# A decoder layer in split fp32: up blocks split in one piece, another order of pairs and plain blocks, and a pair's sums moved back by a unit

## The chip, the cores and the metric

The kernel runs on one core of one Trainium2 chip. The metric is the device time of one execution in microseconds; the median of three runs stands for a kernel. The profile shows one further execution, taken with the hardware profiler.

## The reference

One layer of a causal decoder with 256 tokens and 1024 channels in fp32: three attention mixers are merged, followed by a residual layer norm, a feed-forward part and a second layer norm. Only the feed-forward part and what lies around it bear on this change:

```python
x = layer_norm(ALPHA * x + merged @ w_out[i], ln1_g[i], ln1_b[i])
h = jnp.square(jax.nn.relu(x @ w_up[i])) @ w_down[i]        # w_up 1024 x 4096, w_down 4096 x 1024
ple = jax.nn.sigmoid(x @ w_ple_gate[i]) * (p[i] @ w_ple[i])
x = layer_norm(ALPHA * x + h + ple, ln2_g[i], ln2_b[i])
```

## The kernel before

**Split numbers.** Every fp32 matrix is written as a high part, rounded by a copy to fp32r, and a low part, the rest. A product is three matmuls: high by high, high by low, low by high. A *unit* is a piece of 128 rows by up to 1024 columns of weights. `Weights._split` loads it to a tile `raw` (SyncE's queue), ScalarE casts it to `whi`, and VectorE (for the later units of the kernel alone) subtracts to get `wlo`. There are five buffers each of `raw`, `whi` and `wlo`; `W.get(i)` asks for the splits up to four units ahead of the one that TensorE is about to use.

**The up stage (`for f in range(32)`).** For each of the 32 blocks of 128 hidden channels TensorE does eight matmuls of 512 columns with `whi` as the stationary operand (L929) and eight of 256 columns with `wlo` (L932). VectorE adds the parts (L913), ScalarE applies relu and square, and the result is split into `hT[f]`. The parts of an up unit lie in their tiles at columns given by `UP`: `(16, 192, 320, ...)` for `whi` and `(64, 208, 336, ...)` for `wlo`. The first block of 128 columns stands away from the seven others, so `Apart.runs` gives two runs, and the cast (L109) and the subtraction (L122) of a unit are two instructions each, of 256 and 768 columns.

**The down stage.** The 32 row blocks of `w_down` are used in the order `SEQ`, then `LATE` (26 to 31). Seven *pairs* of row blocks, the tuples of `SEQ`, go through a scheme with seven products in place of eight; the other blocks are *plain*. A plain block is one unit, four products, 12 matmuls of 512 columns. A pair is four units (three of 1024 columns, one of 512), seven products, 21 matmuls. Its units are not all weights as loaded: `load(i)` brings the two row blocks of pair `i` into half of `xr` by three DMAs (L882, L884), and `form(i)` makes the sums and differences by three VectorE instructions (L891 with 1024 columns, L892 and L893 with 512) into `wt[i]` and `xr`. The pair's four units are then split from `wr[i][:, 1]`, `wt[i][:, 0:1024]`, `wr[i][:, 0]` and the last 512 columns of `wt[i]` (L111 and L118). So the second unit needs `form(i)`, the first doesn't. `xr` takes the place of `x1`, the input of the up stage, and has room for two pairs; `load(i + 2)` must wait until pair `i` has been split. It is asked for through the list `later`, when the last unit of pair `i` is split, and `form(i + 2)` is written right behind it.

**The end.** Eight accumulators `P[1]` to `P[8]` collect the products. Behind block 23 VectorE adds them up (`plus`, L1003); meanwhile TensorE does half of the products of blocks 24 and 25 (onto `P[3]` and `P[2]`). The other half goes onto `P[4]` and `P[8]`, and can start when these adds are done. Then come the blocks of `LATE` and the second layer norm.

**Order.** A planner orders each engine's instructions by readiness and program order under its own estimate of durations. `tc.issue_after(x)` keeps what is written in its block behind instruction `x` in the order of `x`'s engine.

Of the kernel before, what the change touches and what calls it, by code (L numbers as in the profile page):

```python
# [142 lines left out]
def hybrid_layer(ctx: ExitStack, tc: tile.TileContext, x0, xn, pT, wqk, wva, wvb, wg, wbc, wba,  # L143
# [12 lines left out]
    W = Weights(tc, raw, part)  # L156
# [75 lines left out]
    def add(*a, at=(0, 0), by=DV):  # L232
        i = n_u[0]
        n_u[0] += 1
        return W.add(*a, by=by if i < 58 else "v", at=at)
# [400 lines left out]
    u_out += [add(wout[4 + i], 1024, wo[:, i, 0], wo[:, i, 1]) for i in range(4)]  # L636
    u_ple = [add(wple[i], 1024) for i in range(2)]
    u_pg = [add(wpg[i], 1024) for i in range(8)]
    UP = (16, *range(192, 1088, 128)), (64, *range(208, 1104, 128))
    u_up = [[add(wup[i], 1024, at=UP)] for i in range(32)]  # L640

    H = (slice(0, 512), slice(512, 1024))
# [206 lines left out]
    for b in range(2):  # L849
        for c in range(2):  # L850
# [3 lines left out]

    SEQ = ((0, 1), 2, 3, (4, 5), 6, 7, (8, 9), 10, (11, 12), 13, (14, 15), 16, (17, 18), 19,
           (20, 21), 22, 23, 24, 25)
    LATE = range(26, 32)
    PAIRS = [k for k in SEQ if isinstance(k, tuple)]  # L860
    hT, at, room = {}, 0, 0
    for k in (*SEQ, *LATE):
        i = PAIRS.index(k) if k in PAIRS else -1
# [14 lines left out]
    def load(i):  # L878

        wr[i] = r = xr[:, i % 2] if i else p3.tile([128, 2, D], F32, name="rows", tag="rows")  # L880
        k1, k2 = PAIRS[i]
        nc.sync.dma_start(r[:, 0], wdn[k1])  # L882
        for h in range(2):
            nc.sync.dma_start(r[:, 1, H[h]], wdn[k2, :, H[1 - h]])  # L884

    def form(i):

        t = p3.tile([128, 2, D], F32, name="rows", tag="rows") if i % 2 else Y
        wt[i] = t = t.rearrange("p b d -> p (b d)")
        r = wr[i].rearrange("p b d -> p (b d)")  # L890
        dve.tensor_tensor(t[:, 0:1024], r[:, 512:1536], r[:, 0:1024], op=ALU.subtract)  # L891
        dve.tensor_tensor(r[:, 512:1024], r[:, 1024:1536], t[:, 0:512], op=ALU.subtract)  # L892
        dve.tensor_tensor(t[:, 1024:1536], r[:, 1536:2048], r[:, 512:1024], op=ALU.subtract)  # L893
# [4 lines left out]
            later.append(i + 2)  # L898
        return r

    later = []
    u_dn = {}
    for k in (*SEQ, *LATE):
        if k in PAIRS:
            i = PAIRS.index(k)
# [54 lines left out]
    xr = p3.tile([128, 2, 2, D], F32, name="xr", tag="x1")  # L960
    for i in (1, 2):
        load(i)
        form(i)

# [7 lines left out]

    def weights(u):
        w = W.get(u)
        while later:
            i = later.pop(0)
            load(i)
            form(i)  # L980
        return w

    def plain(k, w, ids, end=False):
# [6 lines left out]
    TERMS = ((2, 2, 1), (3, 6, 0)), ((7, 5, 1), (5, 3, 0)), ((1, 0, 0), (6, 4, 1)), ((4, 1, 0),)  # L990
    for k in SEQ[:-2]:
        if k not in PAIRS:
            plain(k, weights(u_dn[k][0]), (3, 2, 4, 8), k == 23)
            continue
        for u, terms in zip(u_dn[k], TERMS):
            hi, lo = weights(u)
            for i, a, c in terms:
                a = slice(128 * a, 128 * a + 128)
                onto(i, (hT[k][:, 0, a], hT[k][:, 1, a]), (wide(hi, H[c]), wide(lo, H[c])),
                     k == PAIRS[-1] and i in (1, 5, 6, 7))  # L1000
# [172 lines left out]
```

## Time and profile before

| | |
|---|---|
| median of 3 runs | 417.43 us (417.17 to 418.43) |
| profiled execution | 419.21 us, span in the trace 417.4 us |
| TensorE busy | 405.0 us (97%) |
| VectorE busy | 350.4 us (84%) |
| ScalarE busy | 277.4 us (66%) |
| granted clock over the span | 0.994 |

The span runs from the first to the last instruction of the trace; the time of the execution holds 1.8 us more. A matmul's busy time in the trace is longer than the distance to the next one, as matmuls are pipelined; the pace is read from the distances of their starts.

### The profile page before, as it was taken

The numbers are of one execution on the slowest core, as the hardware profiler recorded it, in microseconds if no ns is written. First come the engines' busy times: TensorE is split into PE (matmuls) and PEld (weight loads), VectorE is DVE, ScalarE is ACT, GpSimd is POOL, SyncE is SP. The second block draws the span as 40 slices with busy tenths as digits, with TensorE's granted clock in tenths as the row PEclk, the third lists the DMA queues.
The fourth block names the chain that finished last, engine by engine and source line by source line (L and its number), as shares of the span: only waits on it lengthen the run. The fifth ranks groups of instructions, "written<-read, shape, count | busy, mean of one in ns | idle before, by whom it ended". The sixth has DMA issues, their size and how long they took to land.

```text
span 417.4 us, 7828 instructions
## 1 busy us (share of the span) xinstructions
PE 405.0 (97%) x2804; PEld 373.5 (89%) x2804; DVE 350.4 (84%) x650; ACT 277.4 (66%) x530; POOL 120.7 (29%) x128
## 2 busy tenths in 40 slices
PE   8999999999999999999999999999999999999993
PEld 8989999998999999999887889999999988788883
DVE  4968769896777789889978889999999798999856
ACT  6877476495798885867415567887889766467310
POOL 1678456174353657500000002433430000000001
PEclk9999999999999999999999999999999999999997
DMA  7896866566474408478980676786576377656502
GB/s 288 292 311 163 310 165 207 167 207 241 136 218 135 133 8 285 125 220 262 336 305 8 226 278 202 236 278 190 197 209 199 103 276 226 184 169 204 200 2 101
DMA packets 27964, 83.49 MB, mean 200 GB/s; under 512 B 3184, under 2 KB 6792, under 8 KB 27540
## 3 DMA queue, kind: packets, MB, share of 16 engines
q1 hardware_dynamic: 27216, 80.46, 59.5%
q10 hardware_dynamic: 612, 2.46, 1.7%
q8 instruction: 22, 0.36, 0.4%
q14 instruction: 18, 0.15, 0.1%
q0 software_dynamic: 96, 0.06, 0.0%
HBM read 81.88 MB, written 1.09 MB: 199 GB/s over the span
## 4 chain that ended last, share of the span: by engine, by line
PE 72%; DVE 12%; DMA 8%; issue 4%; ACT 2%; POOL 1%; SPq 0%; DVEq 0%; ACTq 0%; POOLq 0%
PE mm L188 31%; PE b L188 16%; PE mm L929 13%; PE mm L932 7%; DMA xr<-in_wdn_dram 3%; DVE wlo L118 3%; PE b L370 3%; DMA raw<-in_wva_dram 2%; DVE wlo L122 2%; DMA relt<-in_pick_dram 1%; DMA G<-in_x_dram 1%; PE b L412 1%; PE b L419 1%; ACT whi L111 1%; DVE G L698 1%
## 5 line engine op out<-in xcount | busy, mean ns | idle before, releaser
L111 ACT CAST whi<-raw 128x1024 fp32r<-128x1024 f32 (+3 forms) x92 | 89.4, 987 | 35.4 <-PE b L188 14.6
L122 DVE TENSOR_TENSOR wlo<-raw,whi 128x256 fp32r<-128x256 f32 (+3 forms) x118 | 96.2, 839 | 14.8 <-ACT whi L111 11.5
L188 PE MATMUL mm<-xh,whi 128*128 128x256 f32 x336 | 89.1, 278 | 0.0
L122 POOL TENSOR_TENSOR wlo<-raw,whi 128x384 fp32r<-128x384 f32 (+1 forms) x50 | 68.2, 1375 | 66.7 <-ACT whi L111 59.6
L188 PE MATMUL mm<-xl,whi 128*128 128x256 f32 x336 | 87.1, 277 | 0.0
L188 PE MATMUL mm<-xh,wlo 128*128 128x256 f32 x336 | 79.4, 278 | 0.0
L188 PEld LDWEIGHTS mm<-xh,whi 128*128 128x128 f32 x336 | 64.4, 192 | 0.9
L188 PEld LDWEIGHTS mm<-xl,whi 128*128 128x128 f32 x336 | 64.5, 192 | 0.2
L929 PE MATMUL mm<-x,whi 128*128 128x512 f32 x256 | 60.7, 379 | 0.0
L188 PEld LDWEIGHTS mm<-xh,wlo 128*128 128x128 f32 x336 | 58.7, 192 | 0.2
L188 PE MATMUL b<-whi,store 128*128 128x512 f32 x168 | 52.6, 380 | 0.7 <-DVE store L704 0.4
L929 PEld LDWEIGHTS mm<-x,whi 128*128 128x128 f32 x256 | 46.1, 190 | 5.2
L118 DVE TENSOR_TENSOR wlo<-raw,whi 128x1024 fp32r<-128x1024 f32 (+2 forms) x38 | 43.7, 1170 | 4.0 <-ACT whi L111 3.9
L746 POOL TENSOR_TENSOR rs<-rs,half 128x1 f32<-128x1 f32 x4 | 2.2, 556 | 144.0 <-DVE rs L745 144.0
L109 ACT CAST whi<-raw 128x256 fp32r<-128x256 f32 x64 | 36.4, 612 | 6.1 <-PE b L188 3.7
L188 PEld LDWEIGHTS b<-whi,store 128*128 128x128 f32 x168 | 31.7, 189 | 5.7 <-DVE store L704 0.8
L932 PEld LDWEIGHTS mm<-x,wlo 128*128 128x128 f32 x256 | 33.5, 191 | 1.7
L932 PE MATMUL mm<-x,wlo 128*128 128x256 f32 x256 | 33.8, 275 | 0.0
L188 PE MATMUL b<-wlo,store 128*128 128x512 f32 x84 | 32.2, 383 | 0.6 <-DVE wlo L118 0.6
L953 POOL TENSOR_TENSOR a<-a 128x128 f32<-128x128 f32 x7 | 7.3, 1044 | 57.1 <-ACT a L915 51.5
L188 PE MATMUL mm<-op,whi 128*128 128x256 f32 x128 | 22.1, 278 | 0.0
L188 PE MATMUL b<-whi,x 128*128 128x512 f32 x64 | 19.9, 385 | 0.1
(221 smaller groups left out, 818.6 us busy)
## 6 DMA issues: line engine op xcount, KB each, us to landing
raw<-in_wup_dram SPq DMA_DIRECT2D x32, 512.0 KB, 4.3
raw<-in_wg_dram SPq DMA_DIRECT2D x24, 512.0 KB, 4.4
raw<-in_wqk_dram SPq DMA_DIRECT2D x18, 512.0 KB, 5.7
raw<-in_wdn_dram SPq DMA_DIRECT2D x18, 512.0 KB, 4.5
raw<-in_wout_dram SPq DMA_DIRECT2D x8, 512.0 KB, 4.6
raw<-in_wpg_dram SPq DMA_DIRECT2D x8, 512.0 KB, 6.5
T<-tabd SPq DMA_DIRECT2D x24, 128.0 KB, 3.7
xr<-in_wdn_dram SPq DMA_DIRECT2D x6, 512.0 KB, 3.6
```

Of the source, the lines that this page charges most:

```text
L109: i = nc.scalar.copy(blocks(hi, a, b), blocks(r, a, b))
L111: i = nc.scalar.copy(hi, r)
L118: i = e.tensor_tensor(lo[:, x], r[:, x], hi[:, x].bitcast(F32), op=ALU.subtract)
L122: i = e.tensor_tensor(blocks(lo, *x), blocks(r, *x), blocks(hi, *x).bitcast(F32), op=ALU.subtract)
L188: i = pe.matmul(ps, lhsT=a[x], rhs=b[y], start=first and n == 0, stop=last and n == 2, skip_group_check=more)
L370: m = pe.matmul(ss[2 * n + h][:, QC[b]], lhsT=q[d, x, c], rhs=k[d, y, 0:128 * (b + 1)], start=i == 0, stop=i == 2)
L412: pe.transpose(t[:, 128 * i:128 * i + 128], P[:, 128 * i:128 * i + 128], ident)
L419: pe.matmul(v[:, 256 * i:].rearrange("p (m c q) -> p m c q", c=64, q=2), lhsT=V[:, i, vh], rhs=pt[:, b0:b1].rearrange("p b a (q c) -> p (b ...
L698: dve.scalar_tensor_tensor(o, o, 1.0, order(ps[:, f]), op0=ALU.add, op1=ALU.mult)
L929: pe.matmul(ps, lhsT=hi[:, c], rhs=x1[:, :, k].rearrange("p b a t -> p a t b"), start=k == 0, stop=False)
L932: pe.matmul(ps[:, 0], lhsT=lo[:, c], rhs=x1[:, :, k, 0].rearrange("p b t -> p t b"), start=False, stop=k == KT - 1)
L953: pool.tensor_tensor(sums[2], a11, a21, op=ALU.subtract)
```

## The change

Three things. The up units lie in one piece at columns 64 (`whi`) and 80 (`wlo`); blocks 1 to 7 stay at the columns at which they were, block 0 moves, and the cast and the subtraction are one instruction of 1024 columns each. In `SEQ` the plain blocks stand otherwise: 3, 2, 1, 1, 1, 1, 1 of them behind the seven pairs in place of 2, 2, 1, 1, 1, 1, 2. Which block has which number doesn't count otherwise; the places of `hT` in its tiles follow `SEQ`. And `form(i)` isn't written at once behind `load(i)`: it is written one call of `weights` later, in VectorE's order behind the newest subtraction; `form(1)` and `form(2)`, which stood ahead of the down stage, come with its third and fourth unit.

```diff
-    UP = (16, *range(192, 1088, 128)), (64, *range(208, 1104, 128))
+    UP = 64, 80
     u_up = [[add(wup[i], 1024, at=UP)] for i in range(32)]
...
-    SEQ = ((0, 1), 2, 3, (4, 5), 6, 7, (8, 9), 10, (11, 12), 13, (14, 15), 16, (17, 18), 19,
-           (20, 21), 22, 23, 24, 25)
+    SEQ = ((0, 1), 2, 3, 6, (4, 5), 7, 10, (8, 9), 13, (11, 12), 16, (14, 15), 19, (17, 18), 22,
+           (20, 21), 23, 24, 25)
...
-    later = []
+    later, formed = [], [0, 0, 1, 2]
...
     for i in (1, 2):
         load(i)
-        form(i)
...
     def weights(u):
         w = W.get(u)
+        for i in formed[:1]:
+            formed.pop(0)
+            if i:
+                with tc.issue_after(W.subs[-1]):
+                    form(i)
         while later:
-            i = later.pop(0)
-            load(i)
-            form(i)
+            load(later[0])
+            formed.append(later.pop(0))
         return w
```

## Rows read from the trace of the kernel before

**Rows 1.** The page, busy time (share of the span) and instructions of each engine.
```profile
PE 405.0 (97%) x2804; PEld 373.5 (89%) x2804; DVE 350.4 (84%) x650; ACT 277.4 (66%) x530; POOL 120.7 (29%) x128
```
**Rows 2.** Windows: length, busy of PE, PEld, DVE, ACT, POOL, clock, DMA.
```profile
245.70:329.11 83.41, 83.41 (x512) 76.61 (x511) 80.31 (x126) 70.04 (x149) 21.50 (x28) 1.00 0.64 199
...
363.16:376.98 13.82, 13.82 (x66) 12.09 (x64) 13.75 (x15) 7.88 (x10) 0.00 (x0) 1.00 0.55 166
```
**Rows 3.** Timeline of TensorE in the up stage: start, us, line, operation, count.
```profile
263.61 1.89 PE L929 MATMUL mm<-x,whi 128*128 128x512 f32 x8
265.33 1.05 PE L932 MATMUL mm<-x,wlo 128*128 128x256 f32 x8
266.23 1.89 PE L929 MATMUL mm<-x,whi 128*128 128x512 f32 x8
```
**Rows 4.** Groups of instructions from 245.7 to 329.1: busy, mean ns, idle before.
```profile
L122 DVE TENSOR_TENSOR wlo<-raw,whi 128x768 fp32r<-128x768 f32 x28 | 28.1, 1003 | 0.0
...
L122 DVE TENSOR_TENSOR wlo<-raw,whi 128x256 fp32r<-128x256 f32 x28 | 12.4, 441 | 0.0
```
**Rows 5.** Timeline of TensorE in the down stage, with idle before and its releaser.
```profile
329.11 0.38 PE L188 MATMUL b<-whi,X 128*128 128x512 f32 x1
...
357.63 0.48 PE L188 MATMUL b<-wlo,more 128*128 128x512 f32 x1 [0.32 <-DVE wlo L118]
...
362.84 0.48 PE L188 MATMUL b<-wlo,store 128*128 128x512 f32 x1 [0.56 <-DVE wlo L118]
...
391.93 0.48 PE L188 MATMUL b<-whi,store 128*128 128x512 f32 x1 [0.27 <-DVE b L1003]
```
**Rows 6.** Timeline of TensorE in the last blocks, 512 and 256 columns.
```profile
403.06 2.32 PE L188 MATMUL b<-xw,store 128*128 128x512 f32 x10
...
405.22 0.38 PE L188 MATMUL b<-whi,store 128*128 128x512 f32 x1
...
407.62 0.83 PE L188 MATMUL mm<-xw,store 128*128 128x256 f32 x6
...
408.29 0.28 PE L188 MATMUL mm<-whi,store 128*128 128x256 f32 x1
```
**Rows 7.** Timeline of VectorE in the down stage, with idle before and its releaser.
```profile
334.39 1.23 DVE L891 TENSOR_TENSOR rows<-xr 128x1024 f32<-128x1024 f32 x1 [0.97 <-DMA xr<-in_wdn_dram]
...
352.56 1.22 DVE L118 TENSOR_TENSOR wlo<-raw,whi 128x1024 fp32r<-128x1024 f32 x1
355.21 1.23 DVE L891 TENSOR_TENSOR Y<-xr 128x1024 f32<-128x1024 f32 x1 [1.43 <-DMA xr<-in_wdn_dram]
356.35 1.22 DVE L118 TENSOR_TENSOR wlo<-xr,whi 128x1024 fp32r<-128x1024 f32 x1
357.49 1.22 DVE L118 TENSOR_TENSOR wlo<-rows,whi 128x1024 fp32r<-128x1024 f32 x1
358.62 0.69 DVE L892 TENSOR_TENSOR xr<-xr,Y 128x512 f32<-128x512 f32 x1
359.23 1.22 DVE L118 TENSOR_TENSOR wlo<-xr,whi 128x1024 fp32r<-128x1024 f32 x1
360.36 0.69 DVE L118 TENSOR_TENSOR wlo<-rows,whi 128x512 fp32r<-128x512 f32 x1
360.96 0.69 DVE L893 TENSOR_TENSOR Y<-xr 128x512 f32<-128x512 f32 x1
361.57 1.22 DVE L118 TENSOR_TENSOR wlo<-raw,whi 128x1024 fp32r<-128x1024 f32 x1
```
**Rows 8.** Timeline of SyncE's queue: the DMA issue that completes the fifth pair.
```profile
350.87 0.33 SPq L882 DMA_DIRECT2D xr<-in_wdn_dram  x1
```
**Rows 9.** Timeline of VectorE at the end of the pairs.
```profile
381.84 3.49 DVE L118 TENSOR_TENSOR wlo<-raw,whi 128x1024 fp32r<-128x1024 f32 x3
...
388.91 2.35 DVE L118 TENSOR_TENSOR wlo<-raw,whi 128x1024 fp32r<-128x1024 f32 x2
391.18 0.69 DVE L1003 TENSOR_TENSOR b<-b,Y 128x512 f32<-128x512 f32 x1
```

## Prediction

> **What bounds the kernel now.** I read the page first, then windows over the up and the down stage, then TensorE's timeline, and last VectorE's at the places where TensorE waited. TensorE is busy 97% of the span [rows 1], so time can only come back where it stands still. In the up stage it doesn't: one block of hidden channels begins at 263.61 and the next at 266.23, which is 2.62 us for 8 matmuls of 512 and 8 of 256 columns [rows 3]. From 245.70, where the up stage takes TensorE for itself, to the first matmul of the down stage at 329.11 [rows 2, 5] it is 83.41 us, 31.8 times 2.62 for 32 blocks of which the first has begun. So there is no stall in 83 us, although VectorE is busy 80.31 of them [rows 2].
>
> In the down stage the stalls are counted by starts. Ten matmuls of 512 columns take 405.22 - 403.06 = 2.16 us, 0.216 each [rows 6]. From 329.11 to the matmul at 391.93 [rows 5] the program has 7 pairs of 21, 10 plain blocks of 12 and the first 12 of blocks 24 and 25: 279 matmuls, 60.3 us. They took 62.82, so 2.55 us are stalls; a matmul behind a stall shows 0.48 in place of 0.38 [rows 5], so the last one costs 0.1 more, and 2.65 us is all that can be had before the end. Two kinds of them are seen [rows 5]: TensorE waits for a `wlo` of L118 (at 357.63 and 362.84, and in smaller pieces up to 377), and at 391.93 for an add of L1003. The latter is 0.5: 0.27 idle behind a matmul that counts 0.38 for its 0.216, and 0.1 after it. The others are 2.1.
>
> Why the `wlo` come late is in VectorE's timeline [rows 7]. At 355.21 it starts the fifth pair's sums (L891) after 1.43 us of idleness until their DMA; behind it, at 356.35, stands the first subtraction of the fourth pair, which needs nothing of that DMA and which TensorE is already waiting for (it ends at 357.57; TensorE goes on at 357.63). From then on VectorE works without a break (13.75 of 13.82 us, [rows 2]) and TensorE meets it again and again. VectorE's price by starts: 1.14 for 1024 columns, 0.60 for 512 [rows 7]. A pair costs it 3 x 1.14 + 0.60 for the splits and 1.14 + 2 x 0.60 for the sums, 6.4 us; a plain block 1.14. TensorE needs 21 x 0.216 = 4.54 and 12 x 0.216 = 2.59. A pair and one plain block: VectorE 7.5, TensorE 7.1. So in the stretch with one plain block behind a pair VectorE loses 0.4 us a round, and what it had lost to the DMA doesn't come back.
>
> **The change part by part.**
>
> *Up units in one piece.* A unit's subtraction falls from 1.003 + 0.441 [rows 4] to 1.22 us [rows 7]: 0.22 less, 7 us over 32 units on VectorE; ScalarE has an instruction less a unit too, and is busy 70.04 of the 83.41 us [rows 2]. All of it lies beside a TensorE that never waits there: worth 0 in this stage. It helps only if VectorE enters the down stage ahead, and five buffers cap that at the first five units; the next pair's data can't come, as `xr` lies where `x1` is read until 329. I count 0 for it, at most what it leaves to the later stalls.
>
> The first blocks move by 48 and 16 columns, and TensorE reads them as stationary operands. From below: the pace of 256 columns is (408.29 - 407.62) / 6 = 0.112 [rows 6] with other operands at other places, and in the up stage 8 x 0.216 + 8 x 0.112 = 2.62 is just what is measured [rows 3]; nothing is left to gain. From above: if the load of the moved first block no longer hid under the matmul before, each unit would pay a refill like the one behind a stall, 0.10 us [rows 5], 3.2 us for 32. I take 0, since the two paces are the same for all operands shown, and keep 3.2 as a rival.
>
> *The order.* Work on both engines is the same in sum: the same 7 pairs and plain blocks. What moves are the times at which TensorE comes to them. Before, the second to seventh pair begin 9.72, 19.44, 26.57, 33.70, 40.82 and 47.95 us behind 329.11 if nothing stalls (4.54 a pair, 2.59 a plain block); after, each begins 2.59 later, with one more plain block ahead. VectorE has one more plain split to do for that, 1.14. So at every pair from the second on it has 1.45 us more slack.
>
> *Sums a unit later.* The same three instructions, the same DMAs, none added. What moves is the place in VectorE's queue: at least one subtraction now stands ahead of them. The DMA that completes the fifth pair is issued at 350.87 [rows 8], right behind the last split that reads its place, and the sums could start at 355.21: 4.34 us. Of these 1.43 were idle; with one more split of 1.14 in front of the wait 0.29 would be left, if that split can run. It can't always: it waits for one of five buffers, which TensorE frees. That is a new wait, and behind it on VectorE stand the sums, then the splits of the next pair. Bounds: 0 and the 1.43 of today. Behind the third unit of the down stage the sums of the second pair can't be early either, as they wait for their DMA as before: they start at 334.39 [rows 7], 5.3 us into the stage; with its splits up to the second unit 1.14 + 1.2 + 2 x 1.14 = 4.6 us later it is ready at 9.9, and TensorE comes there at 12.31 + 1.30 = 13.6 (11.0 before). Even the third pair's sums in between (2.34) fit.
>
> Here a rule of the Trainium skill can be set against the row. By SBUF — State Buffer, The DMA setup-cost knee, a transfer takes about 2 us plus its bytes by 436 GB/s, an estimate of 3.2 us for 512 KB. The trace has 4.34 at that place [rows 8, 7], with the issue of the DMA in it, so it doesn't bear the rule out here. By 3.2 no sums would wait and the sum would be 0.2 less.
>
> *The end.* Behind the last pair one plain block stands in place of two before blocks 24 and 25. The adds onto `P[4]` had 2 x 2.59 + 2.59 = 7.8 us behind the last pair and have 5.2. They begin at 391.18, behind two splits of blocks from 26 on (388.91) and, earlier, three more (381.84) [rows 9]. Those three were VectorE's arrears, and most of them should be done by then: 1.45 + 1.43 less arrears. Bounds: 0, and 0.5 + 2.59 = 3.1 if the adds come as far behind the last pair as before. I take 0.5, as today.
>
> **The sum.** Arrears that made 2.1 us of stalls, less 1.45 of slack, less 0.7 (half of 1.43) of idleness: 0, with 0.2 left for what the planner does otherwise. The end stays at 0.5. Gain: 2.1 - 0.2 = 1.9. The profiled execution took 419.21 for a span of 417.4; a span of 415.5 would give 417.3 in its terms. It was 0.4% above the median, and 417.43 - 1.9 = 415.5; I say 415.6.
>
> **The rivals.**
>
> *The wait moves.* The sums stand behind a split that waits for a buffer, or their DMA is as late as before, and VectorE again stands still at several pairs with no plain block to make it up. For it: the loss of 0.4 a round [rows 7], 1.6 over four rounds, just what the slack is. Against: 1.45 of slack ahead of each pair. One such wait of 1.43 and its refills leave 1 to 1.5 us of stalls: 416.3 to 417.2, within the 0.3% (1.25 us) that measurement can tell from no change. Chance 0.19.
>
> *The end takes it.* The adds hang behind splits with 2.59 less cover: up to 2.6 us more at 391, where TensorE waits for L1003 already [rows 5]. 1.9 less 1 to 2.6: 416.4 to 418.1. Against: VectorE comes there with less arrears. Chance 0.10.
>
> *The moved block costs.* 32 loads not hidden at 0.10 us: 3.2 less 1.9, so 418.8. Slower than before from 0.06 us a unit on; in the trace it would be a pace above 2.62 us a block. For it speaks only that the block stood apart; against it that the paces are equal everywhere. Chance 0.07.
>
> *No sums wait at all.* If every pair's data are there when the split in front of its sums ends, which asks for 4.34 less 1.43 plus 1.14, so 4.05 us from issue to start [rows 8, 7], no `wlo` is late and the stalls go to the last one: 417.43 - 2.65 = 414.8, or 415.3 with the end as today. For it: a split of 1.14 is now in front. Against: 4.34 is 0.29 too long at the one place shown. Chance 0.05. The Trainium skill's estimate of 3.2 us, from SBUF — State Buffer as above, would give this.
>
> *Another order elsewhere.* The planner sees shorter splits and may order the up stage or the last blocks otherwise; plus or minus 1 us, mostly the loss of a place that was in tune. 416.5 to 419. Chance 0.07.
>
> **How the numbers follow.** The forecast, 415.0 to 416.4, has 0.52, nearly all of it (0.48) beyond 0.3%, below 416.2. Faster: 0.48 + 0.05 = 0.53. Same: 0.04 of the forecast, 0.19, 0.09 of the end and 0.03 of the last: 0.35. Slower: 0.07, 0.04 of the last and 0.01 of the end: 0.12. The range goes from 414.8, where no stall is left, to 417.8, which takes in the two waits; outside are the moved block and part of the last.
>
> **What would show it.** Up stage: still 2.62 us a block, VectorE's busy time there lower by some 7 us, with one subtraction and one cast of 1024 columns. Down stage: still 279 matmuls up to the first one onto `P[4]`; from its first matmul to that one 60.3 us and at most 1 us of stalls in place of 62.8, with no idleness of VectorE until a DMA of more than 0.5 us ahead of a split that TensorE waits for. The wait for L1003 stays below 1 us. Wrong would be: a pace above 2.62; a VectorE that stands idle for ScalarE's cast ahead of sums that were ready; a longer wait at the adds.

## The result: slower, by 0.8%

The changed kernel takes 421.06 us in the median of seven runs (419.41 to 422.20); the kernel before, on the same chip, 417.43 (417.16 to 419.23). The ratio is 1.0080, with a 95% interval of 1.0064 to 1.0095. Forecast were 415.6 us, with a range from 414.8 to 417.8: a gain was expected and a loss came.

The profiled execution of after took 419.57 us and is one of its quickest, that of before took 419.21 and is one of its slowest, so the spans differ by only 0.4 us. The difference between these two executions lies ahead of the changed part: in the chains that ended last the same 64 matmuls onto `b`, 14.08 us of them, start at 200.09 in after and at 202.81 in before, and TensorE's order is the same up to there. It is a difference between executions: after_pin, after_tail and after_late (below) have the order of after on every engine up to the end of the up stage, and their down stages start at 327.25, 328.15 and 328.13 us. So the two are compared from an event on: the first matmul of the down stage, 326.11 in after and 329.11 in before.

First the page of after, busy time and instructions of each engine, as in [rows 1]:

```profile
PE 403.5 (97%) x2804; PEld 373.0 (89%) x2804; DVE 345.9 (83%) x618; ACT 275.2 (66%) x498; POOL 120.5 (29%) x128
```

VectorE has 4.5 us less to do and 32 instructions less, as the diff promises; TensorE has the same 2804. Then TensorE's timeline in the up stage of after, as in [rows 3]:

```profile
246.62 1.05 PE L932 MATMUL mm<-x,wlo 128*128 128x256 f32 x8
...
249.24 1.05 PE L932 MATMUL mm<-x,wlo 128*128 128x256 f32 x8
```

Still 2.62 us a block (249.24 - 246.62). So nothing has happened here. Now the last stretches, cut at the same events in both kernels: the first matmul of the down stage, the first one onto `P[4]`, the start of TensorE's last one, the end. Windows of before (length, then busy time of PE, PEld, DVE, ACT, POOL, the clock, the DMA share and its GB/s):

```profile
329.11:391.93 62.82, 61.66 (x281) 51.98 (x279) 58.78 (x65) 38.55 (x44) 0.00 (x0) 1.00 0.67 219
391.93:410.19 18.26, 18.26 (x102) 16.49 (x102) 11.72 (x18) 2.94 (x3) 0.55 (x1) 1.00 0.11 40
410.19:417.40 7.21, 0.27 (x3) 0.08 (x1) 3.31 (x8) 0.47 (x1) 1.27 (x2) 0.66 0.30 109
```

and of after:

```profile
326.11:389.05 62.94, 61.52 (x282) 52.21 (x280) 57.38 (x64) 40.13 (x47) 0.00 (x0) 1.00 0.66 217
389.05:407.36 18.31, 18.31 (x102) 16.42 (x102) 9.68 (x13) 2.94 (x3) 0.00 (x0) 1.00 0.08 30
407.36:417.80 10.44, 0.28 (x3) 0.08 (x1) 6.83 (x15) 0.47 (x1) 1.82 (x3) 0.68 0.28 100
```

Two things are to be seen. The first stretch didn't get shorter (62.82, now 62.94), so the forecast gain of 1.9 isn't there. And behind TensorE's last matmul it is 10.44 us to the end in place of 7.21: 3.23 us of loss in a stretch in which TensorE does nothing. With 0.12 and 0.05 from the other two it is 3.4, against 3.6 between the medians. VectorE is busy 6.83 of the last 10.44 us, 3.31 of 7.21 before: work that lay beside TensorE now lies behind it.

**What that work is.** VectorE's timeline at the end, before:

```profile
391.79 0.69 DVE L1003 TENSOR_TENSOR b<-b,a 128x512 f32<-128x512 f32 x1
...
393.51 0.76 DVE L1003 TENSOR_TENSOR mm<-b,a 128x256 f32<-128x256 f32 x2
394.18 0.69 DVE L1003 TENSOR_TENSOR b<-b,Y 128x512 f32<-128x512 f32 x1
...
404.77 1.35 DVE L739 BATCH_NORM_STATS2 st<-b 128x6 f32<-128x512 f32 x2 [4.50 <-PE b L188]
```

and after (L1006 is L1003 of before):

```profile
388.30 0.69 DVE L1006 TENSOR_TENSOR b<-b,Y 128x512 f32<-128x512 f32 x1
388.90 0.68 DVE L1006 TENSOR_TENSOR a<-Y 128x512 f32<-128x512 f32 x1
389.50 2.35 DVE L118 TENSOR_TENSOR wlo<-raw,whi 128x1024 fp32r<-128x1024 f32 x2
391.77 0.76 DVE L1006 TENSOR_TENSOR mm<-b,a 128x256 f32<-128x256 f32 x2
392.44 0.69 DVE L1006 TENSOR_TENSOR b<-b,Y 128x512 f32<-128x512 f32 x1
393.04 0.69 DVE L1006 TENSOR_TENSOR b<-b,a 128x512 f32<-128x512 f32 x1
...
405.81 1.30 DVE L739 BATCH_NORM_STATS2 st<-b 128x6 f32<-128x512 f32 x2 [3.98 <-PE b L188]
```

The add onto `P[8]` is the one of `b<-b,a`; of the two of `b<-b,Y` the first is onto `P[4]`, the second onto `P[2]`. Before, those onto `P[4]` (391.18, [rows 9]) and `P[8]` (391.79) stood together, ahead of those onto the accumulators of the second 128 tokens (`mm<-b,a` and `P[2]`). Now `P[4]` comes at 388.30, but `P[8]` last of all, at 393.04. `P[4]` and `P[8]` hold the first 128 tokens, whose layer norm (L739 and on) is meant to run while TensorE finishes the second 128. It begins 75.66 us behind the start of the down stage before (404.77 - 329.11) and 79.70 after (405.81 - 326.11): 4.0 later. TensorE's timeline in after shows what it did in the meantime:

```profile
392.23 0.38 PE L188 MATMUL b<-whi,store 128*128 128x512 f32 x1
392.45 0.27 PE L188 MATMUL mm<-whi,store 128*128 128x256 f32 x1
...
394.45 0.38 PE L188 MATMUL b<-whi,store 128*128 128x512 f32 x1
...
405.17 1.46 PE L188 MATMUL b<-xw,store 128*128 128x512 f32 x6
406.47 1.17 PE L188 MATMUL mm<-xw,store 128*128 128x256 f32 x9
```

From 392.45 to 394.45 it does 18 of the 36 products of 256 columns, those of the second 128 tokens, ahead of what `P[8]` needs. Before, 32 of the 36 stood behind it: from 405.22 on ([rows 6]) 39 matmuls, 5.1 us, came behind the last one onto `P[4]` or `P[8]`; now 11, the last 2 of the line at 405.17 and the 9 behind it, 1.4 us. TensorE never waits, and yet the time is lost: the layer norm of the first half begins 1.55 us ahead of TensorE's last matmul (405.81 and 407.36), in place of 5.42 in before (404.77 and 410.19), and the rest of it lies behind. ScalarE shows that the weights of the last blocks come later as well: their cast waits for a buffer that TensorE still reads. ScalarE's timeline of before:

```profile
395.69 1.05 ACT L111 CAST whi<-raw 128x1024 fp32r<-128x1024 f32 x1 [5.53 <-PE b L188]
```

The same cast in after:

```profile
397.25 1.05 ACT L111 CAST whi<-raw 128x1024 fp32r<-128x1024 f32 x1 [9.22 <-PE b L188]
```

**Why the down stage gained nothing.** VectorE's timeline of after, at the place that answers to [rows 7]:

```profile
338.89 1.22 DVE L118 TENSOR_TENSOR wlo<-xr,whi 128x1024 fp32r<-128x1024 f32 x1
340.03 0.68 DVE L893 TENSOR_TENSOR Y<-xr 128x512 f32<-128x512 f32 x1
340.63 0.68 DVE L118 TENSOR_TENSOR wlo<-rows,whi 128x512 fp32r<-128x512 f32 x1
341.23 2.35 DVE L118 TENSOR_TENSOR wlo<-raw,whi 128x1024 fp32r<-128x1024 f32 x2
345.31 1.23 DVE L891 TENSOR_TENSOR rows<-xr 128x1024 f32<-128x1024 f32 x1 [1.73 <-issue]
...
349.33 1.22 DVE L118 TENSOR_TENSOR wlo<-xr,whi 128x1024 fp32r<-128x1024 f32 x1
...
354.26 1.22 DVE L891 TENSOR_TENSOR Y<-xr 128x1024 f32<-128x1024 f32 x1 [1.38 <-DMA xr<-in_wdn_dram]
...
363.80 1.23 DVE L891 TENSOR_TENSOR rows<-xr 128x1024 f32<-128x1024 f32 x1 [0.83 <-DVE wlo L118]
```

and SyncE's queue, the issues that complete these pairs, as in [rows 8]:

```profile
340.14 0.33 SPq L882 DMA_DIRECT2D xr<-in_wdn_dram  x1
...
350.57 0.33 SPq L882 DMA_DIRECT2D xr<-in_wdn_dram  x1
...
360.13 0.33 SPq L882 DMA_DIRECT2D xr<-in_wdn_dram  x1
```

From issue to the first sum it is 5.17, 3.69 and 3.67 us, and VectorE stands idle for 1.73, 1.38 and 0.83 of them, where the forecast had 0.29 left of 1.43. The name behind an idle time is inferred: `issue` at the first says that none was found, but the view of tile `xr` from 336 to 347 has a longest landing of 5.1 us behind the issue, and for the issue at 340.14 that is 345.2: this idle time, too, ended with its transfer. Each issue comes right behind the split that frees its place: 340.14 behind the one that starts at 338.89, 350.57 behind the one at 349.33. The chain that ended last runs through the first two of these transfers. TensorE waits as it did, for `wlo`, as in [rows 5]; the longest such wait:

```profile
360.16 0.48 PE L188 MATMUL mm<-wlo,more 128*128 128x512 f32 x1 [0.61 <-DVE wlo L118]
```

The wait for the add at `P[4]`, where the forecast put the danger, has all but gone: some 0.1 us.

### The profile page after: what moved, and what is told of

Read it like the earlier page. It is cut to its first block, busy times and chain, and to the rows that moved or that the text cites. A ratio compares the mean times of both kernels' runs of the same rounds, so it can differ in the third digit from the quotient of the medians.

```text
span 417.8 us, 7771 instructions
## 1 busy us (share of the span) xinstructions
PE 403.5 (97%) x2804; PEld 373.0 (89%) x2804; DVE 345.9 (83%) x618; ACT 275.2 (66%) x498; POOL 120.5 (29%) x128
## 4 chain that ended last, share of the span: by engine, by line
PE 81%; DVE 12%; issue 4%; DMA 2%; ACT 0%; DVEq 0%; POOL 0%; POOLq 0%
PE mm L188 35%; PE b L188 16%; PE mm L929 13%; PE mm L932 7%; PE b L370 3%; DVE wlo L118 3%; PE b L522 3%; DMA xr<-in_wdn_dram 2%; PE b L412 1%; DVE wlo L122 1%; PE b L419 1%; DVE rows L891 1%; PE b L179 1%; DVE store L118 1%; DVE xr L892 1%
## 5 line engine op out<-in xcount | busy, mean ns | idle before, releaser
L111 ACT CAST whi<-raw 128x1024 fp32r<-128x1024 f32 (+3 forms) x124 | 122.3, 999 | 42.0 <-PE b L188 19.6
L118 DVE TENSOR_TENSOR wlo<-raw,whi 128x1024 fp32r<-128x1024 f32 (+2 forms) x70 | 83.0, 1200 | 8.0 <-ACT whi L111 7.5
L122 DVE TENSOR_TENSOR wlo<-raw,whi 128x640 fp32r<-128x640 f32 (+2 forms) x54 | 52.0, 969 | 12.8 <-ACT whi L111 11.5
L953 POOL TENSOR_TENSOR a<-a 128x128 f32<-128x128 f32 x7 | 3.9, 561 | 54.8 <-ACT a L915 54.8
L188 PEld LDWEIGHTS mm<-op,whi 128*128 128x128 f32 x128 | 18.8, 192 | 0.3
```

The lines of the kernel that those rows point to most:

```text
L111: i = nc.scalar.copy(hi, r)
L118: i = e.tensor_tensor(lo[:, x], r[:, x], hi[:, x].bitcast(F32), op=ALU.subtract)
L122: i = e.tensor_tensor(blocks(lo, *x), blocks(r, *x), blocks(hi, *x).bitcast(F32), op=ALU.subtract)
L188: i = pe.matmul(ps, lhsT=a[x], rhs=b[y], start=first and n == 0, stop=last and n == 2, skip_group_check=more)
```

## The experiments

**Theory A**: there are two faults, independent of each other. One block fewer behind the last pair makes the planner put the add onto `P[8]` last, TensorE takes the second 128 tokens' products first, and the first half's layer norm falls behind TensorE's end (some 3.3 us). And in the new order the sums still stand too early for their transfers, so the down stage gains nothing. **Rivals**: the moved up blocks cost; pairs that stand later cost by themselves, wherever; the later sums cost; the stalls belong to the new order, whatever is done about the sums. The letters of the rivals in the expectations hold for the run at hand.

The table has all runs. The kernel before was timed beside each group of runs, so it has several medians, and each ratio is to its own. Columns 4 to 6 are cut from each profile at the events used above (us from the first down-stage matmul to the first onto `P[4]`, from there to the last matmul's start, from there to the end).

| run | median, us | ratio to before (95%) | to `P[4]` | to last | to end |
|---|---|---|---|---|---|
| before | 417.43 to 417.87 | | 62.82 | 18.26 | 7.21 |
| after | 421.06 | 1.0080 (1.0064 to 1.0095) | 62.94 | 18.31 | 10.44 |
| up_only | 417.74 | 1.0006 (0.9995 to 1.0018) | 62.67 | 18.25 | 7.24 |
| seq_only | 421.77 | 1.0102 (1.0084 to 1.0120) | 62.59 | 18.31 | 10.57 |
| form_only | 416.91 | 0.9986 (0.9974 to 0.9997) | 61.91 | 18.25 | 7.25 |
| after_pin | 418.91 | 1.0030 (1.0018 to 1.0043) | 63.38 | 19.75 | 7.23 |
| seq_front | 417.64 | 1.0003 (0.9993 to 1.0014) | 62.84 | 18.26 | 7.20 |
| seq_end | 420.85 | 1.0081 (1.0066 to 1.0096) | 61.84 | 18.15 | 10.56 |
| after_tail | 417.36 | 0.9998 (0.9988 to 1.0008) | 63.34 | 18.15 | 7.25 |
| after_tail_late | 414.53 | 0.9942 (0.9924 to 0.9960) | 60.22 | 18.15 | 7.22 |
| after_late | 418.51 | 1.0018 (1.0005 to 1.0030) | 60.22 | 18.15 | 10.44 |
| no_seq_late | 417.04 | 0.9989 (0.9974 to 1.0004) | 62.01 | 18.25 | 7.24 |
| no_seq_tail_late | 416.17 | 0.9959 (0.9944 to 0.9974) | 60.93 | 18.15 | 7.24 |

**The three parts alone.** Each is one hunk of the diff put into the kernel before: `UP` (up_only), `SEQ` (seq_only), the later `form` (form_only).

> Before, with the up units in one piece and nothing else. Theory A (the loss is made at the end: with the new order of the blocks TensorE takes the products of the second 128 tokens' sums ahead, the first 128 tokens' sums are done later, and only some 1.4 us of matmuls are left beside their layer norm in place of 5.2): this part keeps the old order at the end, so 417.4 us, within 0.3% of before, and 2.62 us a block in the up stage. Rival B (the moved first block, or the longer single instructions, cost): 418.7 or more. A gain beyond 0.3% would say that VectorE's 7 us less work reach the end.

> Before, with the new order of pairs and plain blocks and nothing else. Theory A: all of the loss is here, 420.4 to 421.4 us (0.7 to 0.95% over before), and the matmuls of the second 128 tokens left behind the last one of the first 128 last some 1.4 us. Rival C (the loss comes with the sums written a unit later, which wait behind a split): within 0.3% of before, or faster by the 1.45 us of slack that was forecast.

> Before, with the pairs' sums written a unit later and nothing else. Theory A: the end keeps its order (4.9 us of matmuls behind the first 128 tokens' sums), so within 0.4% of before, 416.5 to 418.7; VectorE still waits for the DMA in front of the fifth pair's sums, by 0.3 to 1.4 us. Rival C: 419 or more.

The whole loss comes with `SEQ`: up_only can't be told from before; seq_only is slower by 1.02%, a little more than expected, and has 10.57 us from TensorE's last matmul to the end. form_only is faster by a hair. In the old order the later sums do what was forecast, and more than expected of this run: the sums of the fourth and fifth pair start at once, with no idle time until their transfers. VectorE's timeline of form_only:

```profile
346.38 1.22 DVE L891 TENSOR_TENSOR rows<-xr 128x1024 f32<-128x1024 f32 x1
...
353.87 1.22 DVE L891 TENSOR_TENSOR Y<-xr 128x1024 f32<-128x1024 f32 x1
```

and SyncE's queue in it, the issues for these two:

```profile
341.28 0.33 SPq L882 DMA_DIRECT2D xr<-in_wdn_dram  x1
...
349.90 0.33 SPq L882 DMA_DIRECT2D xr<-in_wdn_dram  x1
```

From issue to sum it is 5.10 and 3.97 us, about as long as in after, but filled: five and four VectorE instructions stand in between, in place of the three and two of after for the same pairs.

**The order of TensorE held by hand.** after_pin is the changed kernel with the products of the second 128 tokens held behind the first's in the last loop:

```diff
-                     False, k == 31, more=True)
+                     False, k == 31, hold=b == 1, more=True)
```

> The changed kernel with one edit: in the last loop the first matmul of each product for the second 128 tokens is held in program order, so that all of them come behind those of the first 128 tokens (7.9 us of matmuls behind the last one of the first 128). Theory A: the loss goes, 416.5 to 418.2 us, if the wait for the adds onto P[8] that the early products filled doesn't come back in full; it can be up to 2.6 us, and then 419. Rival (the loss is somewhere else in the down stage): 420.5 to 421.5 as the changed kernel.

TensorE now waits for the late add, and the tail is 7.23 again:

```profile
395.36 0.48 PE L188 MATMUL b<-whi,store 128*128 128x512 f32 x1 [1.17 <-DVE b L1006]
```

So the planner had filled a hole of some 1.3 us, and the filling cost 3.2. Of the 0.80% of loss 0.30% stay, 1.25 us, about the size of this wait. The add onto `P[8]` is as late here as in after, and behind this wait TensorE doesn't wait for anything, the weights of the last blocks included: what cost the tail was the order of TensorE's products.

**Where in `SEQ`.** seq_front moves a plain block at the front alone, seq_end takes one from behind the last pair alone. Plain blocks behind the seven pairs: 3,1,1,1,1,1,2 and 2,2,1,1,1,2,1.

```diff
-    SEQ = ((0, 1), 2, 3, (4, 5), 6, 7, (8, 9), 10, (11, 12), 13, (14, 15), 16, (17, 18), 19,
+    SEQ = ((0, 1), 2, 3, 6, (4, 5), 7, (8, 9), 10, (11, 12), 13, (14, 15), 16, (17, 18), 19,
```

```diff
-    SEQ = ((0, 1), 2, 3, (4, 5), 6, 7, (8, 9), 10, (11, 12), 13, (14, 15), 16, (17, 18), 19,
-           (20, 21), 22, 23, 24, 25)
+    SEQ = ((0, 1), 2, 3, (4, 5), 6, 7, (8, 9), 10, (11, 12), 13, (14, 15), 16, (17, 18), 19, 22,
+           (20, 21), 23, 24, 25)
```

> The kernel before with one plain block (6) moved ahead of the second pair and one kept behind the last: SEQ's plain runs are 3,1,1,1,1,1,2. Everything behind the last pair is as in the kernel before. Theory A (the loss is made behind the last pair): TensorE's order of the products behind the sums stays (39 products, some 5.1 us, behind the last onto P[4] and P[8]) and the time stays within 0.3%, 416.3 to 418.7 us. Theory B (pairs that stand later cost by themselves, wherever): some six sevenths of the loss of the order alone, 420.5 to 421.5 us.

> The kernel before with one plain block (22) taken from behind the last pair alone: the runs are 2,2,1,1,1,2,1, every earlier pair stands as before. Theory A (the loss is made behind the last pair): all of the loss of the order alone, 420.3 to 421.8 us (+0.7 to +1.05%), with only some 11 products (1.4 us) behind the last onto P[4] and P[8], the first layer norm's first statistics some 79.5 us after the down stage's start instead of 75.6, and 10.4 us instead of 7.2 from the last product to the end. Theory B (each pair costs where it stands later): a seventh of the loss, 417.6 to 418.3 us.

Both came out as Theory A has it: nothing at the front (1.0003), and 0.81% at the end, where the whole order has 1.02 (the two intervals overlap). seq_end's last two windows show it, TensorE without a break and 10.56 us behind it:

```profile
391.04:409.19 18.15, 18.15 (x103) 16.38 (x101) 9.21 (x13) 2.94 (x3) 0.00 (x0) 1.00 0.06 24
409.19:419.75 10.56, 0.27 (x3) 0.08 (x1) 6.83 (x15) 0.47 (x1) 1.82 (x3) 0.62 0.28 101
```

seq_front says one thing more: a plain block more ahead of the second pair leaves the way to `P[4]` at 62.84. The slack that the forecast saw in it buys nothing by itself.

**Both faults mended, one at a time and together.** after_tail is the changed kernel with the splits of blocks 26 and later queued behind the add onto `P[8]` (no split of them is asked for earlier, and `W.after` is what a split is put behind):

```diff
-        w = W.get(u)
+        w = W.get(u, min(AHEAD, u_dn[25][0] - u))
...
-    plus(P[8], P[8], v35)
+    added = dve.tensor_tensor(P[8], P[8], v35, op=ALU.add)
...
+    W.after = (added.ins,)
     ws = {k: W.get(u_dn[k][0], min(AHEAD, 31 - k)) for k in LATE}
+    W.after = ()
```

after_late gives the sums, from the fourth pair's on, three calls of `weights` later in place of one:

```diff
-            formed.append(later.pop(0))
+            formed.extend((0, 0, later.pop(0)))
```

after_tail_late has both.

> The changed kernel with one thing more: the splits of blocks 26 and later are written and queued behind the add onto P[8], so that TensorE's order behind the sums is again that of the kernel before (38 products, some 5.3 us, behind the last onto P[4] and P[8]); the order of the pairs and the later sums stay. Theory A: the first statistics come again some 75.5 us after the down stage's start and the tail is 7.2 us again; only the waits on VectorE's DMA idleness of the new order remain: 416.5 to 418.2 us. Theory B (the new order costs by its stalls in the down stage or by its end in whatever arrangement): 419.5 us or more.

> As the run before, and a pair's sums given three calls of weights later instead of one, so that they never stand ahead of their transfer's landing. Theory A (two independent faults: the end, and sums that are still given too early in the new order): VectorE's idle time for a DMA ahead of the sums is gone in every pair, the waits of the down stage fall from 2.9 to some 1 us and the time is that of the forecast, 415.0 to 416.5 us. Rival C (the waits of TensorE come from the new order itself, from the splits that stand late whatever VectorE waits for): no faster than the run before, 416.5 to 418.2 us. Theory B: 419 us or more.

> The changed kernel with a pair's sums given three calls of weights later instead of one, and its end as it stands (11 products, 1.44 us, behind the last onto P[4] and P[8]). Theory A (two independent faults): the down stage's waits fall from 2.9 to under 0.5 us, the end keeps its loss (10.4 us from the last product to the end, first statistics some 79 us after the down stage's start less what the waits gave): 417.8 to 419.0 us. Rival D (the late end takes whatever the down stage gains, as the layer norm waits for something other than TensorE): 420 us or more.

The four corners add up. The end mended takes 0.82 points off the ratio with the sums as they are (1.0080 to 0.9998) and 0.76 with them later (1.0018 to 0.9942); the later sums take 0.62 and 0.56. In us of 417.5 that is some 3.3 for the end and 2.5 for the sums. The rivals of these runs fall: the stalls don't belong to the new order, as the first stretch of after_tail_late and of after_late has none left at all, and the late end of after_late doesn't take what the down stage gains. Windows of after_tail_late, same cuts:

```profile
326.61:386.83 60.22, 60.22 (x282) 52.74 (x280) 57.57 (x65) 40.44 (x47) 0.00 (x0) 1.00 0.68 227
386.83:404.98 18.15, 18.15 (x103) 16.38 (x101) 13.24 (x19) 3.04 (x3) 0.55 (x1) 1.00 0.14 44
404.98:412.20 7.22, 0.27 (x3) 0.08 (x1) 3.31 (x8) 0.47 (x1) 1.27 (x2) 0.77 0.30 109
```

Busy and length of TensorE are equal in the first two rows. In its VectorE timeline five instructions, four of them splits, stand between the issue for the fifth pair at 349.06 on SyncE's queue and the sum at 354.16, and no idle time is noted. The last three and the sum:

```profile
350.76 1.22 DVE L118 TENSOR_TENSOR wlo<-raw,whi 128x1024 fp32r<-128x1024 f32 x1
351.89 1.22 DVE L118 TENSOR_TENSOR wlo<-xr,whi 128x1024 fp32r<-128x1024 f32 x1
353.03 1.22 DVE L118 TENSOR_TENSOR wlo<-rows,whi 128x1024 fp32r<-128x1024 f32 x1
354.16 1.22 DVE L891 TENSOR_TENSOR Y<-xr 128x1024 f32<-128x1024 f32 x1
```

Idle time in itself isn't what costs: at the fourth pair VectorE still idles 0.27 us here and 1.04 in after_late, and TensorE doesn't wait. What it waited for in after were splits that stood behind the sums on VectorE; more of them now stand ahead. This version beats both kernels, and its expected range: 414.53 us, 0.58% below the kernel before (0.40 to 0.76%).

**Is the new order of any use?** The same with the order of before: no_seq_late (`UP` and sums three calls later), no_seq_tail_late (the queue at the end as well).

> The changed kernel with the order of blocks of the kernel before (2,2,1,1,1,1,2), and a pair's sums given three calls later; the end as it then falls out (37 products, 4.9 us, behind the last onto P[4] and P[8]). Theory A with a new order that has a use of its own (a plain block more between the late sums and their pair): the sums stand right ahead of the pair that needs them, some waits of TensorE stay, 0.7 us or more at the pairs and some 1.0 at the add onto P[4], 415.8 to 417.2 us. Rival E (the new order has no use at all): only the wait at P[4]'s add stays, 414.8 to 415.7 us.

> As the run before, with the splits of blocks 26 and later behind the add onto P[8] as well (45 products, 6.4 us, behind the last onto P[4] and P[8]): the best version so far without its new order. Theory A: 1 us or more above the version with the new order (414.5), 415.4 to 416.8 us. Rival E (the new order has no use at all): the same as that version, 414.0 to 415.1 us.

no_seq_late, 417.04, lies in Theory A's range: 0.8 us of stalls at the second pair and 1.0 at the add onto `P[4]`, no better than form_only. With the end mended some 0.7 us of stalls stay, all at the second pair, which has only two plain blocks ahead of it. So the third block ahead is worth some 0.7 us by the traces. The ratios (0.9959 and 0.9942) say 0.17 points, 0.7 us as well, but their intervals overlap, so by the times alone it isn't settled.

## Why the prediction was wrong

**The end: the step that failed.** It asked only whether the adds would come later than TensorE, took the price from a wait at `P[4]` (0.5, at most 3.1), and rival *The end takes it* did the same. The wait fell to 0.1. What it put at nothing without asking is what the planner does when the add onto `P[8]` comes late: it gives TensorE other work. That kept TensorE busy and took 28 of the 39 matmuls from the place where they covered the first half's layer norm. Measured: 3.2 us in after, 3.3 between the kernels with and without the mended end. *Another order elsewhere* had the kind of mechanism (0.07), but at plus or minus 1 us it had a third of its price. The cover could have been read off the trace of before: VectorE starts the norm at 404.77, TensorE starts its last matmul at 410.19, and 5.4 us of VectorE's chain lie between.

**Sums a unit later, with The order: gained nothing.** Forecast were 1.45 and 0.7 us off arrears that make 2.1 us of stalls; measured is 62.94 for 62.82. The step counted one split of 1.14 in front of the wait and took the rest of the queue as it was in [rows 7]. Alone the part worked (form_only, 0.9 us off the first stretch). With the new order VectorE comes earlier to the fourth pair's sums, 17.5 us into the down stage in place of 19.1 in form_only. The transfer doesn't come earlier, since it waits for the split that frees its place: its issue is 14.0 us into the stage in both. So the slack went into idle time, 1.73 us there; the splits behind the sums came later by that, and with them the next transfer (24.5 us into the stage, 22.6 in form_only). seq_only has the same without the moved sums: 1.89 and 1.85 us of idle time ahead of the fourth and fifth pair's sums, 0.21 and 1.43 in before. That is rival *The wait moves*, at 0.19, and at more than its price: it left not 1 to 1.5 but all 2.7 us of stalls. Two calls later still, the gain is there and larger than forecast: 62.94 to 60.22. The estimate of 3.2 us from the Trainium skill (SBUF — State Buffer, The DMA setup-cost knee) was below the trace again: by it the three sums shown would have idled for 0, 0.9 and 0.4 us in place of 1.73, 1.38 and 0.83.

**What held.** The price list: 60.3 us without a stall for the way to `P[4]` (60.22 measured), so 2.65 us to be had. *Up units in one piece* at nothing: 1.0006, 2.62 us a block; *The moved block costs* falls. VectorE's busy time in the up stage fell by 3.9 us, not 7 (76.42 in the 83.41 us from 242.70 on): the 0.22 a unit was a difference of durations, and the two instructions overlap. From the start of the pair of them at 289.64 in before to the next start it is 1.20 us, and one of 1024 columns takes 1.14. It changed nothing. The forecast gain of 1.9 us would have been about right for a change that also mended the two faults: after_tail_late gains 0.58%, 2.4 us.

**Open.** Why the planner puts the add onto `P[8]` last when one block fewer stands ahead is argued from the order alone: its own estimates stand in no trace. What the traces show is when it does: the add onto `P[8]` is the last one in all five kernels with one block there and the splits of blocks 26 and later where they were (after, seq_only, seq_end, after_pin, after_late), and stands ahead of the second 128 tokens' adds in the other eight. It also stays open why the first 200 us differ by 2.7 us from one execution to another.

## What to carry to other kernels

A change of order near the end is costed not by TensorE's waits alone: name the work that runs beside its last matmuls, and what keeps the order that lets it run there; a planner that fills a hole of 1.3 us can uncover 3.3 us of tail. An engine that gets slack ahead of a transfer turns it into idle time unless what starts the transfer moves as well or more work is put in front of the wait. And when a change of several parts loses, mend the bad part before it is dropped: here the version with all three parts kept and the two faults mended has the lowest median of all.

## What was unexpected

TensorE's time to the end can be shorter and the kernel slower: from the first down-stage matmul to the last one it is 80.0 us in seq_end and 81.1 in before, yet seq_end is slower by 0.81%. And the time from a DMA's issue to the first use of its 512 KB is no constant in one and the same stage: 5.17, 3.69 and 3.67 us in after for three transfers of the same shape, all waited for.
